# Five expert pairs' outputs through DRAM rows instead of one-hot products, and a third weight load under way, in a decoder layer with a mixture of experts

## The chip, the cores and the metric

One core of a Trainium2 chip runs the whole layer as one program. The metric is device time in microseconds: the median of three runs of the kernel before is 706.11 us (704.12 to 707.72). TensorE is called PE here, VectorE DVE, ScalarE ACT, GpSimd POOL, and SyncE, which only issues DMAs, SP.

## The reference, cut to what matters

A decoder layer on 512 tokens of 1024 float32 channels: two attention branches, then a mixture of 32 experts of which each token takes two, then a final norm. The change is in the mixture, of which the reference does this:

```python
g_sel = jnp.argmax(g_logits, axis=-1)            # one of 4 groups
top_vals, top_idx = lax.top_k(e_in, 2)           # two of its 8 experts
weight = p_group * jax.nn.softmax(top_vals, axis=-1)
expert_id = g_sel[:, None] * 8 + top_idx
...
def expert_block(args):                          # the tokens of one expert
    xb, e = args
    return (jax.nn.silu(xb @ w_g[e]) * (xb @ w_u[e])) @ w_d[e]
...
out = jnp.zeros((T, D)).at[slot_tok].add(ys * slot_w[:, None])
```

Each expert has three weights of 1 MB (two of 1024x256, one of 256x1024), so the mixture reads 96 MB. x is then x plus this sum, and the result is its rmsnorm.

## The kernel before, in words

Up to about 436 us the kernel computes the attention branches, their merge and the router. From there `experts` (L819) works through the 32 experts as 16 pairs q = 0 to 15. A pair has 128 slots: 64 partitions for each of its two experts, one row of x per slot. On 512 tokens with two choices over 32 experts, some half of the slots hold a token. In a pair, PE does in this order (the order on PE and POOL is written out by hand, `manual_schedule` at L826; on the other engines a planner sets it):

1. `gate_up` (L760): 32 products for G, 32 for U (line 769), from the transposed rows xT and the two experts' weights. ACT makes silu of G (L774), for which it needs the slot's norm factor r from the small tile sw; DVE multiplies with U into a (L775).
2. `some(5)`: five `combine` calls (L811) that belong to the pair before. A combine is two products of a one-hot matrix S (token by slot, made by `one_hot`, L806) with the pair's outputs y, split in a high and a low part (L815 and L816), and an addition of the 128x512 result to x2 by DVE (L817). A pair has eight: four token tiles t times two halves of the channels.
3. `act_T` (L778): two transposes of a (L781), copied back by ACT (L783).
4. `some(3)`: the other three combines.
5. `next_rows` (L851): eight transposes (L746) of the next pair's gathered rows xg into xT, scaled by ACT (L753) and DVE (L754).
6. `down` (L786): 16 products with the down weights in two halves (L795). Of each half ACT writes the weighted high part (L802) and DVE the low part (L803).

POOL copies the slot weights of a pair into sw (`slot_weights`, L733: two copies of 64 partitions, L738, and one of 128, L739), and after `next_rows` it issues two indirect DMAs (`gather_rows`, L723, line 728) that fetch the rows of pair q + 2: xg, 4 KB for each slot that holds a token, and wg, 132 bytes for each. Slots without a token have an index out of bounds and are skipped. xg has one buffer, so a gather waits until the transposes of the rows before have read it.

The weights come through SP. `new_w` (L669) hands out 20 buffers of 1 MB (NH) in a ring: load n takes the buffer of load n - 20, that is of a weight some three pairs earlier. `load` (L678) also makes load n wait until load n - 2 has landed, so that two are under way. After pair 15, `last` (L876) does its combines, the norm and the store.

The tiles that stay (constants, router results) come from the pool `const`, and small rotating ones from `small`; the pool of big tiles begins in memory behind them.

Of the kernel before, what the change touches and what calls it, by code (L numbers as in the profile page):

```python
# [10 lines left out]
F32 = mybir.dt.float32  # L11
# [3 lines left out]
I32 = mybir.dt.int32  # L15
U32 = mybir.dt.uint32
AF = mybir.ActivationFunctionType
ALU = mybir.AluOpType
# [3 lines left out]
P = 128  # L22
T = 512
NT = T // P
D = 1024
# [5 lines left out]
NEG = -1e30  # L31
NE = 32
NH = 20


class Layer:
# [84 lines left out]
    def setup(self):  # L121
        nc, tc, ctx, io = self.nc, self.tc, self.ctx, self.io
        self.const = ctx.enter_context(tc.tile_pool(name="const", bufs=1, side="left"))
        self.small = ctx.enter_context(tc.tile_pool(name="small", bufs=1, side="left"))
        self.big = ctx.enter_context(tc.tile_pool(name="big", bufs=16, side="left"))
        c = self.const
        self.ident = c.tile([P, P], F32, name="ident")
        make_identity(nc, self.ident)
        self.mhalf = c.tile([P, 1], F32, name="mhalf")
        nc.gpsimd.memset(self.mhalf, -0.5)  # L130
        self.eps = c.tile([P, 1], F32, name="eps")
        nc.gpsimd.memset(self.eps, EPS * D)

    def load_consts(self):
# [495 lines left out]
    def route_setup(self):  # L630
        nc, tc, io, c = self.nc, self.tc, self.io, self.const
        self.dram = dp = self.ctx.enter_context(tc.tile_pool(name="dram", bufs=1, space=bass.MemoryType.DRAM))
        self.x2d = dp.tile([T, D], F32, name="x2d")
        self.Wd = dp.tile([T, NE + 1], F32, name="Wd")
        self.wr = c.tile([P, KD, 40], F32, name="wr")
        nc.gpsimd.memset(self.wr, 0.0)
        self.load_late(self.wr[:, :, 0:4], io["w_router_group"][0].rearrange("(j p) g -> p j g", p=P))
        for g in range(4):
            self.load_late(self.wr[:, :, 8 + 8 * g:16 + 8 * g],
                              io["w_router_expert"][0, g].rearrange("(j p) e -> p j e", p=P))  # L640
        self.gpj = c.tile([P, KD], F32, name="gpj")
        self.load_late(self.gpj, io["ffn_norm"][0].rearrange("(p j) -> p j", p=P))
        self.gcol = gcol = c.tile([P, KD], F32, name="gcol")
        self.load_late(gcol, io["ffn_norm"][0].rearrange("(j p) -> p j", p=P))
        nc.vector.tensor_scalar(self.gpj, self.gpj, 32.0, None, ALU.mult)
        nc.vector.tensor_scalar(gcol, gcol, 32.0, None, ALU.mult)
        nc.vector.tensor_tensor(self.wr, self.wr, gcol.unsqueeze(2).to_broadcast([P, KD, 40]), ALU.mult)
        self.rb = c.tile([P, 40], F32, name="rb")
        nc.gpsimd.memset(self.rb, -3e38)
        self.load_late(self.rb[:, 0:4], io["b_router_group"][0:1, :].to_broadcast([P, 4]))  # L650
        self.load_late(self.rb[:, 8:40], io["b_router_expert"].rearrange("o g e -> o (g e)")
                          .to_broadcast([P, 32]))
        self.rc = c.tile([P, 33 + NT], F32, name="rc")
        self.load_late(self.rc, io["rconst"])
        self.iota32 = self.rc[:, 0:32]
        self.slot = self.rc[:, 32:33]
        self.token = self.rc[:, 33:33 + NT]
        self.tri = c.tile([P, 2, P], F16, name="tri")
        self.after(nc.gpsimd.dma_start(self.tri, io["tri"]), self.started)
        self.tm = c.tile([P, T], F16, name="tm")  # L660
        self.after(nc.gpsimd.dma_start(self.tm, io["tm"]), self.started)
        self.M = c.tile([P, NT, NE], F16, name="M")
        self.sq = c.tile([P, 2, NT], F32, name="sq")
        self.W = c.tile([P, NT, NE + 1], F32, name="W")
        self.iotaU = c.tile([P, NE], U32, name="iotaU")
        nc.vector.tensor_copy(self.iotaU, self.iota32)


    def new_w(self):  # L669
        i = self.nw % NH  # L670
        self.nw += 1
# [5 lines left out]

    def load(self, dst, src):  # L678
        d = self.nc.sync.dma_start(dst, src)
        if len(self.loads) >= 2:  # L680
            self.after(d, self.loads[-2])
        self.loads.append(d)

    def load_w(self, src, how):
# [126 lines left out]
    def combine(self, S, y, half, t):  # L811
# [4 lines left out]
        nc.tensor.matmul(cp, S[:, t * P:(t + 1) * P], y[1], start=False, stop=True)  # L816
        nc.vector.tensor_tensor(self.x2[t][:, hs], self.x2[t][:, hs], cp, ALU.add)  # L817

    def experts(self):  # L819
        nc, tc = self.nc, self.tc  # L820
        NP = NE // 2
        wgu, wd = {}, {}
        for q in range(3):
            wgu[q], wd[q] = self.load_gu(q), self.load_d(q)
        self.yhl = self.wp.tile([P, 2048], F32R, name="yhl", tag="whi")
        with tc.manual_schedule(engines={mybir.EngineType.PE, mybir.EngineType.Pool}):  # L826
            xT, sw, xg = {0: self.xT0}, {}, {}
            S, y, todo = None, None, []
            for q in range(NP):
                if q > 0 and q + 2 < NP:  # L830
                    wgu[q + 2], wd[q + 2] = self.load_gu(q + 2), self.load_d(q + 2)
                    if q + 2 == NP - 1:
                        self.load_final()
                if q:
                    sw[q] = self.slot_weights(q, wg, nc.gpsimd)

                def some(n):
                    for _ in range(min(n, len(todo))):
                        self.combine(S, y[todo[0][0]], *todo[0])
                        todo.pop(0)  # L840

                def between(j):
                    if q == 0 and j == 3:
                        self.tokens()
                        xg[1] = self.gather_rows(self.xi[:, 1:2], self.rows)
                    if q == 0 and j == 5:
                        sw[0] = self.take_weights()
                    if q == 0 and j == 9:
                        self.count_blocks()
                a = self.gate_up(wgu.pop(q), xT.pop(q), lambda: sw[q][1], between)  # L850
                def next_rows():  # L851
                    xT[q + 1] = self.new_xT()
                    for g in range(2):
                        self.gathered_T(xg[q + 1][0], xT[q + 1], g)
                if q == 0:
                    next_rows()
                some(5)
                aT = self.act_T(*a)
                some(3)
                if 0 < q < NP - 1:  # L860
                    next_rows()
                if q + 1 < NP:
                    wg = xg.pop(q + 1)[1]
                if q + 2 < NP:
                    xg[q + 2] = self.gather_rows(self.xi[:, q + 2:q + 3])
                S = self.one_hot(self.xf[:, q:q + 1])
                dn = wd.pop(q)
                y = [None, None]
                todo = [(h, t) for h in range(2) for t in range(NT)]
                if q == NP - 1:  # L870
                    self.last(S, dn, aT, sw[q][0])
                    break
                for h in range(2):
                    y[h] = self.down(dn, aT, sw[q][0], h)
# [158 lines left out]
class Route:  # L1033
# [60 lines left out]
    def choose_experts(self):  # L1094
        nc, L = self.nc, self.L
        self.v8, vi = self.tmp("v8", [8]), self.tmp("vi", [8], U32)
        nc.vector.max(self.v8, self.es)
        nc.vector.max_index(vi, self.v8, self.es)
        self.Mk = self.tmp("Mk", [2, NE])
        nc.vector.tensor_tensor(self.Mk, L.iotaU.unsqueeze(1).to_broadcast([P, 2, NE]),  # L1100
                                vi[:, 0:2].unsqueeze(2).to_broadcast([P, 2, NE]), ALU.is_equal)
        nc.vector.tensor_tensor(L.M[:, self.t], self.Mk[:, 0], self.Mk[:, 1], ALU.add)
# [15 lines left out]

    def places(self):
        nc, L, t, N = self.nc, self.L, self.t, self.N  # L1120
        n = self.tmp("n", [2])
        for c in range(2):
            nc.vector.scalar_tensor_tensor(self.es, self.Mk[:, c], 1.0, N, ALU.mult, ALU.mult, accum_out=n[:, c:c + 1])
        self.at(self.AB[:, :, 0:64], n)
# [33 lines left out]
def shape_consts():  # L1158
    out = {}
# [8 lines left out]
    q = np.arange(P)[:, None]  # L1168
    c = np.arange(T)[None, :]
# [2 lines left out]
    tri[:, 0] = np.arange(P)[:, None] <= np.arange(P)[None, :]  # L1172
    tri[:, 0] += 1024.0 * np.eye(P)
    out["tri"] = tri
    rc = np.zeros((P, 33 + NT), np.float32)
    rc[:, 0:32] = np.arange(32)
    rc[:, 32] = 1025 + np.arange(P) % 64
    rc[:, 33:] = np.arange(P)[:, None] + P * np.arange(NT)[None, :] - 1024
    out["rconst"] = rc
    out["tm"] = np.broadcast_to(np.arange(T, dtype=np.float32) - 1024, (P, T)).copy()  # L1180
    return out
# [30 lines left out]
```

## Time and profile before

| | |
|---|---|
| runs, median of 3 | 706.11 us |
| profiled execution, its own time | 705.33 us |
| its span, first to last instruction | 703.5 us |
| mean granted TensorE clock | 0.992 |
| PE busy | 683.6 us (97%) |
| DVE, ACT, POOL busy | 57%, 39%, 10% |
| DMA moved | 148.17 MB, mean 211 GB/s |

All times inside the trace count from the span's first instruction. The profiled execution's time is 1.83 us over its span, and 0.78 us under the median. A mean duration of matmuls is longer than their spacing, since they overlap: how far apart they start is read from a timeline. The DMA share is the part of the time that packets took on the core's 16 DMA engines; it can pass 1.00 a little, since a packet counts where it starts.

### The profile page before, as it was taken

The numbers are of one execution on the slowest core, as the hardware profiler recorded it, in microseconds if no ns is written. First come the engines' busy times: TensorE is split into PE (matmuls) and PEld (weight loads), VectorE is DVE, ScalarE is ACT, GpSimd is POOL, SyncE is SP. The second block draws the span as 40 slices with busy tenths as digits, with TensorE's granted clock in tenths as the row PEclk, the third lists the DMA queues.
The fourth block names the chain that finished last, engine by engine and source line by source line (L and its number), as shares of the span: only waits on it lengthen the run. The fifth ranks groups of instructions, "written<-read, shape, count | busy, mean of one in ns | idle before, by whom it ended". The sixth has DMA issues, their size and how long they took to land.

```text
span 703.5 us, 11377 instructions
## 1 busy us (share of the span) xinstructions
PE 683.6 (97%) x4262; PEld 522.5 (74%) x4262; DVE 398.8 (57%) x972; ACT 277.3 (39%) x623; POOL 70.9 (10%) x151
## 2 busy tenths in 40 slices
PE   8999999999999999999999999999999999999991
PEld 7998887777788888888888998566656666666651
DVE  5535956877829964423765317255555544555545
ACT  5747544555638663422333334211212111212123
POOL 1404000000000000000000012211121111111103
PEclk9999999999999999999999999999999999999996
DMA  8725431110272144212789758898999999999923
GB/s 256 152 61 90 106 121 60 61 49 13 68 171 61 27 156 119 61 61 94 262 301 352 287 189 315 316 361 308 377 364 393 392 394 355 372 377 348 367 89 122
DMA packets 73786, 148.17 MB, mean 211 GB/s; under 512 B 30938, under 2 KB 53554, under 8 KB 61952
## 3 DMA queue, kind: packets, MB, share of 16 engines
q1 hardware_dynamic: 67616, 138.69, 56.1%
q10 hardware_dynamic: 3040, 4.27, 2.3%
q0 software_dynamic: 3072, 4.46, 2.1%
q8 instruction: 35, 0.57, 0.3%
q14 instruction: 23, 0.19, 0.1%
HBM read 145.35 MB, written 4.26 MB: 213 GB/s over the span
## 4 chain that ended last, share of the span: by engine, by line
PE 88%; DMA 4%; issue 3%; DVE 2%; ACT 1%; POOL 1%; SPq 0%; POOLq 0%; DVEq 0%; ACTq 0%
PE yp L795 7%; PE G L769 6%; PE U L769 6%; PE pacc L96 5%; PE pacc L95 5%; PE pacc L94 5%; PE pacc L448 4%; PE pacc L447 4%; PE pacc L449 4%; PE cp L815 4%; PE cp L816 3%; PE ptr L420 3%; DMA wg<-Wd,xi 3%; PE S L402 2%; PE O L428 2%
## 5 line engine op out<-in xcount | busy, mean ns | idle before, releaser
L65 DVE SCALAR_TENSOR_TENSOR wlo<-wraw,ms,whi 128x256 fp32r<-128x256 f32 (+2 forms) x134 | 68.3, 552 | 31.4 <-ACT whi L64 31.2
L64 ACT ACTIVATE whi<-wraw,ms 128x256 fp32r<-128x256 f32 (+2 forms) x134 | 67.0, 559 | 42.1 <-PE pacc L448 20.1
L817 DVE TENSOR_TENSOR x<-x,cp 128x512 f32<-128x512 f32 x128 | 78.1, 682 | 0.8 <-PE cp L816 0.8
L94 PE MATMUL pacc<-whi,hThi 128*128 128x352 f32 (+1 forms) x192 | 72.6, 378 | 0.0
L95 PE MATMUL pacc<-wlo,hThi 128*128 128x352 f32 (+1 forms) x192 | 70.6, 369 | 0.0
L96 PE MATMUL pacc<-whi,hTlo 128*128 128x352 f32 (+1 forms) x192 | 70.5, 367 | 0.0
L775 DVE SCALAR_TENSOR_TENSOR a<-U,sw,a 128x256 f32<-128x256 f32 x16 | 11.0, 685 | 84.9 <-PE U L769 62.0
L795 PE MATMUL yp<-w,a 128*64 128x512 f32 x256 | 58.5, 598 | 0.5 <-ACT a L783 0.5
L769 PE MATMUL G<-w,xT 128*64 128x256 f32 x512 | 58.3, 380 | 0.0
L769 PE MATMUL U<-w,xT 128*64 128x256 f32 x512 | 58.2, 379 | 0.0
L769 PEld LDWEIGHTS G<-w,xT 128*64 128x64 f32 x512 | 36.5, 137 | 24.6 <-issue 4.6
L815 PE MATMUL cp<-yhl,S 128*128 128x512 f32 x128 | 53.6, 419 | 0.2 <-DVE x L817 0.2
L816 PE MATMUL cp<-yhl,S 128*128 128x512 f32 x128 | 50.8, 396 | 0.8 <-DVE yhl L803 0.8
L447 PE MATMUL pacc<-hThi,whi 128*128 128x512 f32 x128 | 50.6, 396 | 0.0
L448 PE MATMUL pacc<-hTlo,whi 128*128 128x512 f32 x128 | 50.4, 394 | 0.0
L769 PEld LDWEIGHTS U<-w,xT 128*64 128x64 f32 x512 | 36.7, 137 | 18.4
L449 PE MATMUL pacc<-hThi,wlo 128*128 128x512 f32 x128 | 50.1, 392 | 0.0
L415 ACT ACTIVATE E<-E,mx 128x128 f32<-128x128 f32 (+3 forms) x64 | 35.6, 557 | 20.5 <-DVE mx L412 19.7
L803 DVE SCALAR_TENSOR_TENSOR yhl<-yp,sw,yhl 128x512 fp32r<-128x512 f32 x32 | 24.0, 751 | 31.3 <-ACT yhl L802 31.3
L802 ACT ACTIVATE yhl<-yp,sw 128x512 fp32r<-128x512 f32 x32 | 22.0, 687 | 47.4 <-PE yp L795 47.4
L94 PEld LDWEIGHTS pacc<-whi,hThi 128*128 128x128 f32 x192 | 36.1, 188 | 5.2 <-issue 1.3
L95 PEld LDWEIGHTS pacc<-wlo,hThi 128*128 128x128 f32 x192 | 36.1, 188 | 4.5 <-issue 0.7
(221 smaller groups left out, 1307.8 us busy)
## 6 DMA issues: line engine op xcount, KB each, us to landing
w<-in_w_exp_gate_dram SPq DMA_DIRECT2D x32, 1024.0 KB, 6.1
w<-in_w_exp_up_dram SPq DMA_DIRECT2D x32, 1024.0 KB, 6.1
w<-in_w_exp_down_dram SPq DMA_DIRECT2D x30, 1024.0 KB, 5.8
wraw<-in_w_in_dram SPq DMA_DIRECT2D x14, 1024.0 KB, 5.3
wraw<-in_w_out_dram SPq DMA_DIRECT2D x4, 1024.0 KB, 7.1
wraw<-in_w_in_dram SPq DMA_DIRECT2D x5, 704.0 KB, 4.8
xs<-in_x_dram SPq DMA_DIRECT2D x4, 512.0 KB, 6.6
wraw<-in_w_o_mla_dram SPq DMA_DIRECT2D x4, 512.0 KB, 3.4
```

Source lines behind the costliest of these rows:

```text
L65: nc.vector.scalar_tensor_tensor(lo[:, k], raw[:, k], g, hi[:, k].bitcast(F32), ALU.mult, ALU.subtract)
L94: nc.tensor.matmul(ps[t][:, :ncols], act_hi[kk // 4][:, kk % 4, ts], hi[:, k], start=kk == 0, stop=False)
L95: nc.tensor.matmul(ps[t][:, :ncols], act_hi[kk // 4][:, kk % 4, ts], lo[:, k], start=False, stop=False)
L96: nc.tensor.matmul(ps[t][:, :ncols], act_lo[kk // 4][:, kk % 4, ts], hi[:, k], start=False, stop=kk == ktot - 1)
L447: nc.tensor.matmul(ps, hi[:, k, ds], self.hT[0][k // 4][:, k % 4], start=k == 0, stop=False)
L448: nc.tensor.matmul(ps, hi[:, k, ds], self.hT[1][k // 4][:, k % 4], start=False, stop=False)
L449: nc.tensor.matmul(ps, lo[:, k, ds], self.hT[0][k // 4][:, k % 4], start=False, stop=k == KD - 1)
L769: nc.tensor.matmul(GU[i][es, 0:256], xT[:, j, es], gu[e][i][:, j * 256:(j + 1) * 256], start=j == 0, stop=j == KD - 1)
L795: nc.tensor.matmul(yp[es], aT[:, j, es], wd[e][:, j * D + half * 512:j * D + half * 512 + 512], start=j == 0, stop=j == 1)
L815: nc.tensor.matmul(cp, S[:, t * P:(t + 1) * P], y[0], start=True, stop=False)
L816: nc.tensor.matmul(cp, S[:, t * P:(t + 1) * P], y[1], start=False, stop=True)
L817: nc.vector.tensor_tensor(self.x2[t][:, hs], self.x2[t][:, hs], cp, ALU.add)
```

## The change

Pairs 1, 3, 5, 7 and 9 (`VIA`) no longer combine. `down_out` lets ACT write the weighted outputs of both halves into a 128x1024 tile y, and POOL issues a DMA that writes y (512 KB) into its 128 rows of a new DRAM tensor yd. S, the high and low parts and the eight combines of these pairs go. In pairs 10 to 13, `take_slots` fetches, for token tile t = q - 10 and for each of the two choices, the rows of yd that belong to the tile's tokens: POOL fills a 128x1024 tile with zeros and issues an indirect DMA; tokens whose choice is not in those five pairs have an index out of bounds. One pair later, DVE adds the two tiles to x2. The rows' numbers are worked out once by DVE in `slot_rows`, in pair 1, from the router's masks Mk and places, which are now kept for all token tiles in `const`. The combines that are left are spread: in pairs 1 to 10 four of them instead of eight, two ahead of `act_T` and two behind it. A load waits for the load three before it. The constant table rc is longer by 32 columns, and a tile `pad` of 24 floats is put behind `eps`.

```diff
+VIA = (1, 3, 5, 7, 9)
...
+        c.tile([P, 24], F32, name="pad")
...
     def load(self, dst, src):
         d = self.nc.sync.dma_start(dst, src)
-        if len(self.loads) >= 2:
-            self.after(d, self.loads[-2])
+        if len(self.loads) >= 3:
+            self.after(d, self.loads[-3])
...
+    def slot_rows(self):
+        nc, c = self.nc, self.const
...
+        for t in range(NT):
+            for i in range(2):
+                nc.vector.scalar_tensor_tensor(junk, self.Mk[:, t, i], 1.0, self.base, ALU.mult, ALU.mult,
+                                               accum_out=rows[:, t, i:i + 1])
+        nc.vector.tensor_scalar(far, self.place, 1088.5, float(1 << 20), ALU.is_gt, ALU.mult)
+        nc.vector.tensor_tensor(rows, rows, self.place, ALU.add)
+        self.yi = c.tile([P, NT, 2], I32, name="yi")
+        nc.vector.tensor_tensor(self.yi, rows, far, ALU.add)
+
+    def down_out(self, wd, aT, sw, q):
+        nc = self.nc
+        y = self.bl.tile([P, D], F32, name="y", tag="yd", bufs=2)
+        for h in range(2):
+            nc.scalar.mul(y[:, h * 512:h * 512 + 512], self.down_products(wd, aT, h), sw)
+        i = VIA.index(q) * P
+        nc.gpsimd.dma_start(self.yd[i:i + P], y)
+
+    def take_slots(self, t, i):
+        nc = self.nc
+        y = self.bl.tile([P, D], F32, name="y", tag="yd", bufs=2)
+        nc.gpsimd.memset(y, 0.0)
+        nc.gpsimd.indirect_dma_start(out=y, out_offset=None, in_=self.yd,
+                                     in_offset=bass.IndirectOffsetOnAxis(ap=self.yi[:, t, i:i + 1], axis=0),
+                                     bounds_check=len(VIA) * P - 1, oob_is_err=False)
+        return t, y
...
-                some(5)
+                n = min(len(todo), 4) if VIA[0] <= q <= VIA[-1] + 1 else len(todo)
+                some((n + 1) // 2 + (n > 4))
                 aT = self.act_T(*a)
-                some(3)
+                some(n // 2 - (n > 4))
...
                 if q + 2 < NP:
                     xg[q + 2] = self.gather_rows(self.xi[:, q + 2:q + 3])
+                if q == 1:
+                    self.slot_rows()
+                for t, r in taken:
+                    nc.vector.tensor_tensor(self.x2[t], self.x2[t], r, ALU.add)
+                t = q - VIA[-1] - 1
+                taken = [self.take_slots(t, i) for i in range(2)] if 0 <= t < NT else []
+                dn = wd.pop(q)
+                if q in VIA:
+                    self.down_out(dn, aT, sw[q][0], q)
+                    continue
                 S = self.one_hot(self.xf[:, q:q + 1])
```

## Rows read from the trace of the kernel before

**Rows 1.** The page: busy time of PE, then the span in 40 slices of 17.6 us (GB/s of all DMAs), then the queue of POOL's DMAs (packets, MB, share of 16 engines).

```profile
PE 683.6 (97%) x4262; PEld 522.5 (74%) x4262; DVE 398.8 (57%) x972; ACT 277.3 (39%) x623; POOL 70.9 (10%) x151
...
GB/s 256 152 61 90 106 121 60 61 49 13 68 171 61 27 156 119 61 61 94 262 301 352 287 189 315 316 361 308 377 364 393 392 394 355 372 377 348 367 89 122
...
q0 software_dynamic: 3072, 4.46, 2.1%
```

**Rows 2.** PE's timeline of one pair (start us, duration us, engine, line, operation), weight loads left out: the first two and the fifth product of the combines, the transposes of a, the transposes of the next rows, and the down products.

```profile
598.53 0.50 PE L815 MATMUL cp<-yhl,S 128*128 128x512 f32 x1
598.87 0.40 PE L816 MATMUL cp<-yhl,S 128*128 128x512 f32 x1
...
599.57 0.39 PE L815 MATMUL cp<-yhl,S 128*128 128x512 f32 x1
...
600.96 0.38 PE L781 MATMUL G<-ident,a 128*128 128x128 f32 x2
...
602.58 1.31 PE L746 MATMUL ptr<-ident,xg 128*128 128x128 f32 x8
603.82 3.65 PE L795 MATMUL yp<-w,a 128*64 128x512 f32 x16
```

**Rows 3.** The chain that ended last, in order of time: the G products of pair 4 and of pair 15.

```profile
497.73 3.45 PE G L769 x32
...
670.03 3.45 PE G L769 x32
```

**Rows 4.** Stretches of the expert stage: us; busy time of PE, PEld, DVE, ACT, POOL with counts; then granted clock, DMA share, GB/s.

```profile
440.00:460.00 20.00, 19.54 (x148) 12.00 (x145) 7.34 (x18) 4.03 (x8) 3.94 (x7) 1.00 0.90 321
460.00:475.00 15.00, 15.00 (x104) 9.24 (x103) 7.63 (x14) 2.87 (x6) 2.61 (x5) 1.00 0.96 367
475.00:497.50 22.50, 22.29 (x139) 13.04 (x139) 13.40 (x24) 4.79 (x10) 4.85 (x8) 1.00 0.90 329
497.50:655.00 157.50, 157.50 (x1070) 98.83 (x1068) 82.75 (x141) 31.36 (x61) 26.05 (x50) 1.00 0.97 374
655.00:675.30 20.30, 20.30 (x154) 12.92 (x152) 9.03 (x15) 4.89 (x9) 0.84 (x5) 1.00 0.83 310
```

**Rows 5.** Who SP's weight loads waited for: us in total, times, longest.

```profile
SPq L679 <- DMA w<-in_w_exp_gate_dram: 87.9, 28, 8.7
SPq L679 <- DMA w<-in_w_exp_up_dram: 77.4, 29, 5.2
SPq L679 <- DMA w<-in_w_exp_down_dram: 69.4, 29, 3.6
...
SPq L679 <- PE cp L816: 3.0, 12, 0.3
```

**Rows 6.** SP's timeline: the gate loads of pair 4 and of pair 15, and the last load of all (the down weights of pair 15 come in four loads of half the size, this is the fourth).

```profile
453.52 3.59 SPq L679 DMA_DIRECT2D w<-in_w_exp_gate_dram  x2
...
651.30 2.82 SPq L679 DMA_DIRECT2D w<-in_w_exp_gate_dram  x2
...
669.33 0.55 SPq L679 DMA_DIRECT2D w<-in_w_exp_down_dram  x1
```

**Rows 7.** From issue to landing (min, median, max us) of the loads: the very last one, issued at 669.33, and the 66 issued between 459 and 655 us. Then PE's down products of pair 15.

```profile
DMA to landing us min/median/max: 6.0/6.0/6.0
...
DMA to landing us min/median/max: 4.9/5.8/8.8
...
681.02 3.65 PE L795 MATMUL yp<-w,a 128*64 128x512 f32 x16
```

**Rows 8.** Two stretches with the same columns as rows 4: one with up to four loads of 1 MB under way (weights of the experts and of the merge together), and one with two.

```profile
372.40:388.70 16.30, 16.30 (x72) 13.06 (x71) 7.12 (x10) 3.98 (x6) 0.00 (x0) 1.00 0.99 363
...
504.60:514.60 10.00, 10.00 (x56) 6.12 (x56) 7.71 (x14) 2.70 (x6) 2.24 (x3) 1.00 1.01 408
```

**Rows 9.** Timelines of POOL, ACT and DVE around the same pair as rows 2; in brackets the idle time before and what ended it.

```profile
589.71 1.03 POOL L728 DMA_INDIRECT wg<-Wd,xi  x1 [0.30 <-issue]
590.75 0.19 POOL L738 COPY sw<-wg 64x1 f32<-64x1 f32 x1
597.72 0.18 POOL L738 COPY sw<-wg 64x1 f32<-64x1 f32 x1 [6.78 <-DMA wg<-Wd,xi]
597.96 0.18 POOL L739 COPY sw<-wg 128x1 f32<-128x1 f32 x1
...
591.83 0.69 ACT L802 ACTIVATE yhl<-yp,sw 128x512 fp32r<-128x512 f32 x1 [1.06 <-PE yp L795]
598.18 0.72 ACT L774 ACTIVATE a<-G,sw 128x256 f32<-128x256 f32 x1 [5.66 <-POOL sw L739]
...
598.93 0.69 DVE L775 SCALAR_TENSOR_TENSOR a<-U,sw,a 128x256 f32<-128x256 f32 x1 [5.63 <-ACT a L774]
```

**Rows 10.** Groups of instructions (count, busy us, mean ns), and DMA issues (count, KB each, median us to landing).

```profile
L817 DVE TENSOR_TENSOR x<-x,cp 128x512 f32<-128x512 f32 x128 | 78.1, 682 | 0.8 <-PE cp L816 0.8
L475 DVE TENSOR_TENSOR gate<-gate 128x512 f32<-128x512 f32 x8 | 5.5, 688 | 0.1
L619 POOL MEMSET xg<- 128x1024 f32 x1 | 0.9, 947 | 0.0
...
x2d<-x ACTq DMA_DIRECT2D x4, 384.0 KB, 5.4
xg<-x2d,xi POOLq DMA_INDIRECT x15, 6.9
```

More of the change, by code (lines that the diff above doesn't have):

```diff
@@ L633, in route_setup @@
         self.x2d = dp.tile([T, D], F32, name="x2d")
+        self.yd = dp.tile([len(VIA) * P, D], F32, name="yd")
         self.Wd = dp.tile([T, NE + 1], F32, name="Wd")
@@ L652, in route_setup @@
                           .to_broadcast([P, 32]))
-        self.rc = c.tile([P, 33 + NT], F32, name="rc")
+        self.rc = c.tile([P, 33 + NT + NE], F32, name="rc")
         self.load_late(self.rc, io["rconst"])
@@ L657, in route_setup @@
         self.token = self.rc[:, 33:33 + NT]
+        self.base = self.rc[:, 33 + NT:]
         self.tri = c.tile([P, 2, P], F16, name="tri")
@@ L662, in route_setup @@
         self.M = c.tile([P, NT, NE], F16, name="M")
+        self.Mk = c.tile([P, NT, 2, NE], F32, name="Mk")
+        self.place = c.tile([P, NT, 2], F32, name="place")
         self.sq = c.tile([P, 2, NT], F32, name="sq")
@@ L817, in combine @@
         nc.vector.tensor_tensor(self.x2[t][:, hs], self.x2[t][:, hs], cp, ALU.add)
+    def slot_rows(self):
+        nc, c = self.nc, self.const
+        rows = c.tile([P, NT, 2], F32, name="yrows")
+        far = c.tile([P, NT, 2], F32, name="far")
+        junk = c.tile([P, NE], F32, name="yjunk")
+        for t in range(NT):
[21 more added lines that the diff above has]
+        return t, y
     def experts(self):
@@ L827, in experts @@
             xT, sw, xg = {0: self.xT0}, {}, {}
-            S, y, todo = None, None, []
+            S, y, todo, taken = None, None, [], []
             for q in range(NP):
@@ L865, in experts @@
                     xg[q + 2] = self.gather_rows(self.xi[:, q + 2:q + 3])
+                if q == 1:
[8 more added lines that the diff above has]
+                    continue
                 S = self.one_hot(self.xf[:, q:q + 1])
-                dn = wd.pop(q)
                 y = [None, None]
@@ L1098, in choose_experts @@
         nc.vector.max_index(vi, self.v8, self.es)
-        self.Mk = self.tmp("Mk", [2, NE])
+        self.Mk = L.Mk[:, self.t]
         nc.vector.tensor_tensor(self.Mk, L.iotaU.unsqueeze(1).to_broadcast([P, 2, NE]),
@@ L1120, in places @@
         nc, L, t, N = self.nc, self.L, self.t, self.N
-        n = self.tmp("n", [2])
+        n = L.place[:, t]
         for c in range(2):
@@ L1174, in shape_consts @@
     out["tri"] = tri
-    rc = np.zeros((P, 33 + NT), np.float32)
+    rc = np.zeros((P, 33 + NT + NE), np.float32)
     rc[:, 0:32] = np.arange(32)
     rc[:, 32] = 1025 + np.arange(P) % 64
-    rc[:, 33:] = np.arange(P)[:, None] + P * np.arange(NT)[None, :] - 1024
+    rc[:, 33 + NT:] = [64 * (2 * VIA.index(i // 2) + i % 2) - 1025 if i // 2 in VIA else 1 << 20 for i in range(NE)]
+    rc[:, 33:33 + NT] = np.arange(P)[:, None] + P * np.arange(NT)[None, :] - 1024
     out["rconst"] = rc
```

## The prediction, made before the changed kernel ran

> **What bounds the kernel now.** I read the page first: PE is busy 97% of the span, and from slice 24 on the DMAs move 308 to 394 GB/s, more than anywhere before [rows 1]. So the expert stage, the only one that the change touches beyond a few small tiles, has two loads near their limit at once, and the question is which of them sets its end. For PE I read a pair's timeline and the chain: the chain of pairs 4 to 15 is nothing but PE, and a pair takes (670.03 - 497.73) / 11 = 15.66 us [rows 3]. For the DMAs I read SP: the gate loads of pair 4 are issued at 453.52 and those of pair 15 at 651.30, which is 197.78 / 11 = 17.98 us for a pair [rows 6]. So the loads are the slower of the two. They start well ahead, 497.73 - 453.52 = 44.2 us before their products, and end 670.03 - 651.30 = 18.7 us ahead. SP's waits say what holds them: 234.7 us for the landing of another load against 3.0 us for the combines that free a buffer [rows 5]. PE lives on a lead that it uses up at 2.3 us a pair. At the end little is left: the last load lands at 669.33 + 6.0 = 675.3, and its half of the down products begins at 681.02 + 1.83 = 682.85 [rows 6, 7]. **The slack is 7.5 us.** PE cannot end earlier by more than that unless the stream of loads ends earlier too.
>
> **PE's side of the sum.** Removed are 40 combines, 80 products. Within a run of combines the second and the fifth product start at 598.87 and 599.57, so 0.233 us apart (the 0.4 us of a row is longer, since they overlap) [rows 2]. 80 x 0.233 = 18.7 us less, spread as 1.87 us over each of pairs 1 to 10. Nothing is added on PE. The 40 DVE additions that go (0.68 us each) and the new ones (8 of 128x1024, by twice 0.69 us for 128x512 in SBUF, 1.4 us each, 11 us) hang on an engine that is busy 82.75 of 157.50 us [rows 4, 10]; I cost them at nothing, as long as their rows have landed, and a pair passes in between. slot_rows is some eleven short DVE instructions, hidden likewise. The pad, the longer table, Mk and places only move addresses: nothing, and no row could show otherwise.
>
> What comes back on PE are waits for a, and here POOL matters. In the pair shown, U's last products end about when the first combine starts, at 598.53; a is ready at 598.93 + 0.69 = 599.62, and the five combines cover this until 600.96 [rows 2, 9]. With two combines the transposes would want it at 598.53 + 0.94 = 599.47: 0.15 us late, 1.5 us over ten pairs. But POOL was the late one already: its second copy into sw waits 6.78 us, until the gather issued just before it has landed, and only then come silu (0.72) and a [rows 9]. I read this as: that copy waits for everything that POOL has in its queue. Then a write of yd holds it too. Its y is complete at 591.83 + 0.69 = 592.52; POOL's issue lies at once behind; landing after 5.4 us, as 384 KB from ACT's queue took, up to 5.4 x 512 / 384 = 7.2 us [rows 10], so at 598.0 to 599.8 instead of 597.72. With 0.46 us to silu and 1.44 us through silu and a (as in rows 9: 597.72 to 598.18, 598.18 to 599.62), a comes at 599.9 to 601.7, 0.4 to 2.2 us too late. I take 1.3, for five pairs 6.5 us. The fetches: behind wg's issue, which ends at 590.74, two memsets of 0.95 and two issues of 1.03, each with some 0.3 us around it, put the second fetch's issue at about 594.0 and its landing, by 5.4 to 6.9 us, at 599.4 to 600.9; a comes at 601.3 to 602.8, while the five combines of pairs 11 to 14 last until 600.96. That is 0.3 to 1.8 us, I take 1.1, for four pairs 4.4 us. If the copy does not wait for them, both are nothing. **PE's own end moves by -18.7 + 1.5 + 6.5 + 4.4 = -6.3 us**, between -17.2 and -18.7 + 1.5 + 11 + 7.2 = +1.0.
>
> **The loads' side.** Added traffic: five writes of 0.524 MB, 2.62 MB; eight fetches in which only the tokens of ten of the 32 experts move, 1024 x 10 / 32 = 320 rows of 4 KB, 1.31 MB. Together 3.93 MB. At the 374 GB/s of the long stretch [rows 4] this is 10.5 us; at the best stretch's 408 GB/s [rows 8] 9.6 us. It could cost more: today's six loads of a pair, at the best spacing 4.9 / 2 = 2.45 us each [rows 7], would take 14.7 of the 17.98 us, and if all of the other 3.3 us were the doing of the gather, which moves about 4.1 / 15 = 0.28 MB [rows 1], the price would be 12 us for a MB and the sum 46 us. But 363 GB/s also stands in a stretch ahead of the first gather [rows 8], so I take 10.5 and keep up to 20 for the range.
>
> The writes ride on POOL's queue, beside SP's. The Trainium skill's page "DMA: Bandwidth & Descriptors" (section "Issuing engines are not separate DMA queues") has a rule against this part of the change: DMAs of every issuing engine run on the same 16 DMA engines and interleave. The trace agrees, a share of 0.97 over 157.5 us with both queues at work [rows 4]; by the rule the writes cost the loads their bytes, without it writes and fetches would cost the loads nothing, and their sum would be 10.5 us lower.
>
> The third load can only fill what is idle. By the DMA shares that is 20.0 x 0.10 + 15.0 x 0.04 + 22.5 x 0.10 + 157.5 x 0.03 + 20.3 x 0.17 = 13.0 us up to 675.3 [rows 4]. Against much more speaks that up to four loads under way gave 363 GB/s and two gave 408 [rows 8], though those four had shorter pieces; for some speaks that the lowest shares stand where loads are few or small, at 440 to 460 and at the end, where two halves under way are 1 MB. From 0 to 13 I take 7.5. **The last landing then moves by +10.5 - 7.5 = +3.0 us, and with 7.5 us of slack used up PE ends 4.5 us earlier.** That PE frees buffers earlier doesn't help: hardly a wait for a buffer ends last [rows 5].
>
> **Sum.** The later of the two ends counts, the loads' -4.5 against PE's -6.3. The tail behind the down products stays. From the profiled execution's 705.33 us this is 700.8; the median stands 0.78 us above that execution, so I forecast 706.11 - 4.5 = 701.6 us.
>
> **The rivals.**
> *The third load is worth all of the idle time and POOL's copy waits for nothing new.* Then the loads end at -7.5 + 10.5 - 13.0 = -10 us and PE at -17.2, so the kernel at 696. For it: shares of 0.83 and 0.90 in 63 us of the stage. Against it: rows 8, and the copy's wait in rows 9. A stream that is faster still would leave PE's own limit, 706.11 - 17.2 = 689.
> *The traffic wins: slower.* Place: the loads of pairs 12 to 15. If the 13 new transfers cost 20 us and the third load gives nothing, the stream ends 20 us later, PE waits for the down weights of pair 15 and ends +12.5 us: 718.6; it decides from the point where traffic minus the third load's gain exceeds the 7.5 us of slack. Halfway, at 14 and 0, it is 712.6. For it: 0.97 share already. Against: 13 us of idle share.
> *POOL's wait takes the place of the combines.* If landings of writes and fetches take 2 us longer than I took, nine pairs lose 18 us more and PE ends at -6.3 + 18 = +11.7 us, 717.8; at 0.7 us longer it is no change, 706. It would show as idle PE ahead of L781 in pairs 2 to 14. The Trainium skill's "GPSIMD Engine Reference" (section "Specifications") says that GpSimd's port to SBUF is shared with VectorE when a DVE instruction has two SBUF inputs; no row here shows what that costs, and the new additions are of that kind.
> *It does no more than move waits about:* traffic and third load cancel to the 7.5 us of slack, 706.
>
> **Chances.** Forecast (loads set the end, 698 to 706): 0.42, of which 0.28 lie more than 0.5% faster. All of the idle time used: 0.12, faster. Traffic: 0.20, of which 0.14 slower. POOL: 0.16, of which 0.10 slower and 0.02 faster. Nothing: 0.10, of which 0.08 within and the rest to either side. A measurement of this kernel can tell about 0.5%, 3.5 us, from no change. Together: faster 0.43, same 0.32, slower 0.25. The likeliest case's own range is 698 to 706; from the costs' ends (689 and 718) I cut what the tails leave, one in ten on each side: 694 to 712.
>
> **What would show it.** Right: pairs 1 to 10 take about 14 us where nothing waits; SP has three loads under way, and its waits are still for landings; the DMA share over 497 to 655 is nearer 1.0, at no more than some 385 GB/s; PE's idle time lies ahead of G, U or down products in the last four pairs and its releaser is a weight load; the last load lands at about 678. POOL's L738 copies would begin at landings of yd. Wrong: loads that wait for buffers to the end (then PE is the bound and rows 5 misled me); PE idle ahead of L781 for 2 us and more in each pair; a rate well over 400 GB/s in the long stretch (then the third load is worth more); a last landing behind 683 (then it is slower).

## The result and the profile after

The changed kernel takes 713.21 us (median; 711.16 to 713.70) against 705.75 us for the kernel before beside it (704.12 to 707.72): a ratio of 1.0096, with a 95% interval of 1.0067 to 1.0126. It is slower by about 1%, where 701.6 us was forecast. The profiled execution after takes 711.16 us with a span of 709.4 us, 5.83 us over the profiled one of before.

The page of the changed kernel, to be held against [rows 1]: PE's busy time, the granted clock and the GB/s in slices of 17.7 us, and POOL's DMA queue.

```profile
PE 671.5 (95%) x4182; PEld 510.5 (72%) x4182; DVE 376.5 (53%) x944; ACT 277.5 (39%) x623; POOL 91.9 (13%) x172
...
PEclk9999999999999999999999999999999999888997
...
GB/s 256 150 61 89 105 120 60 60 61 1 90 154 54 61 120 119 76 43 118 264 278 381 248 232 271 407 413 415 419 413 411 415 416 415 414 417 358 65 1 122
...
q0 software_dynamic: 4944, 8.35, 3.5%
```

PE is busy 12 us less, with 80 products fewer, and 3.89 MB more go through POOL's queue, as the change says. Two things are new. From slice 26 to 36 the DMAs move 407 to 419 GB/s, where they moved 308 to 394, and then they are done: 65 and 1 GB/s in slices 38 and 39. The loads have finished long before the end. And PE's clock, full over the whole stage before [rows 4], is down in three slices, 35 to 37 (602 to 656 us).

The expert stage of the changed kernel, in the columns of [rows 4]: first the long stretch, then four short ones in pair 11.

```profile
497.50:655.00 157.50, 139.66 (x945) 85.91 (x941) 62.69 (x102) 28.84 (x56) 38.79 (x62) 0.94 1.01 409
...
590.00:598.00 8.00, 8.00 (x64) 5.13 (x60) 0.60 (x1) 0.00 (x0) 2.50 (x4) 1.00 1.02 412
598.00:604.00 6.00, 0.03 (x1) 0.00 (x0) 1.21 (x3) 0.70 (x1) 0.37 (x2) 0.70 1.02 421
604.00:608.00 4.00, 3.88 (x13) 3.14 (x14) 3.60 (x6) 0.38 (x1) 0.00 (x0) 0.60 1.02 424
608.00:612.00 4.00, 4.00 (x23) 1.78 (x24) 3.65 (x7) 1.31 (x3) 2.66 (x2) 1.00 1.00 414
```

PE was busy all 157.50 us of the long stretch before; now 18 us of it are idle. Six of them lie in one piece, from 598 to 604, and in the 4 us behind it the granted clock is 0.60 on average, between its two levels of 1.2 and 2.4 GHz; 13 products start there, and 23 in the 4 us after, at full clock.

What holds PE there is read from the timelines of the four engines at the same place, in the form of [rows 9]; the sixth line is from the view of line 744 (590 to 602 us) and gives the shortest, median and longest time, in ns, that POOL's sequencer spent waiting for a semaphore ahead of a copy.

```profile
587.11 1.00 POOL L734 DMA_INDIRECT wg<-Wd,xi  x1 [0.30 <-issue]
589.35 1.00 POOL L854 DMA_INDIRECT y<-yd,yi  x1 [0.27 <-POOL y L853]
591.58 1.00 POOL L854 DMA_INDIRECT y<-yd,yi  x1 [0.27 <-POOL y L853]
592.59 0.19 POOL L744 COPY sw<-wg 64x1 f32<-64x1 f32 x1
601.59 0.18 POOL L744 COPY sw<-wg 64x1 f32<-64x1 f32 x1 [8.81 <-DMA y<-yd,yi]
...
L744 POOLq EVENT_SEMAPHORE  x2: 17/3122/6227, 594.6 to 595.3; - x2
...
602.06 0.70 ACT L780 ACTIVATE a<-G,sw 128x256 f32<-128x256 f32 x1 [12.24 <-POOL sw L745]
602.79 0.66 DVE L781 SCALAR_TENSOR_TENSOR a<-U,sw,a 128x256 f32<-128x256 f32 x1 [12.19 <-ACT a L780]
603.30 1.86 DVE L823 TENSOR_TENSOR x<-x,cp 128x512 f32<-128x512 f32 x3
...
588.89 3.62 PE L775 MATMUL G<-w,xT 128*64 128x256 f32 x32
...
597.63 0.40 PE L822 MATMUL cp<-yhl,S 128*128 128x512 f32 x1
...
604.12 0.77 PE L821 MATMUL cp<-yhl,S 128*128 128x512 f32 x1 [6.09 <-DVE x L823]
...
612.17 3.62 PE L775 MATMUL G<-w,xT 128*64 128x256 f32 x32
```

Follow it from the top. POOL issues the gather of pair 12 and then the two fetches, the last at 591.58. The second copy into sw, which pair 11 needs, starts only at 601.59, when that fetch has landed, 9.9 us after its issue. This wait is in the program: POOL's sequencer stands 6.23 us in one wait instruction ahead of that copy, and the semaphores for which the trace has the copy wait are those of pair 12's gathers and of both fetches, although it reads none of what they bring; why the program has these waits is open. Silu and a come behind it at 602.06 and 602.79. DVE works in order, and the additions of the combines stand behind a in its queue; four combines (eight products, the last at 597.63) fill the four PSUM tiles into which combines write, and the fifth waits for the first addition, until 604.12. So the combines can't cover a late a beyond the fourth. Then the products of 128x512 follow each other at 0.43 us (606.81 to 607.24 in the trace) instead of 0.233 for 3 us. The pair takes 23.28 us, from the first G product at 588.89 to the next pair's at 612.17, where it took 15.64 before. The next two do the same (23.52 each); the fourth, whose fetches are issued when the loads are over, takes 16.51.

The groups of the changed kernel show the same as sums: the releaser behind the last bar of each line, with the idle time it ended.

```profile
L781 DVE SCALAR_TENSOR_TENSOR a<-U,sw,a 128x256 f32<-128x256 f32 x16 | 10.9, 682 | 125.7 <-ACT a L780 112.7
...
L821 PE MATMUL cp<-yhl,S 128*128 128x512 f32 x88 | 41.0, 466 | 18.2 <-DVE x L823 18.2
...
L780 ACT ACTIVATE a<-G,sw 128x256 f32<-128x256 f32 x16 | 11.4, 712 | 102.2 <-POOL sw L745 96.7
```

Only L821's 18.2 us are PE's, and they are three quarters of the 24 us that these four pairs lose; the idle times of ACT and DVE are long but mostly beside PE's work.

The account of the 5.8 us by which PE's last down products start later (689.90 against 684.08), from the starts of the G products: the experts begin 1.59 us later (437.51 against 435.92), pairs 1 to 10 take 137.37 instead of 157.38 us (-20.01), pairs 11 to 14 take 86.83 instead of 62.56 (+24.27), pairs 0 and 15 the same. So the change wins what it promised in ten pairs, and loses it and more in the four that fetch.

### The profile page after: what moved, and what is told of

It is laid out like the page before. It is cut to its first block, busy times and chain, and to the rows that moved or that the text cites. A ratio compares the mean times of both kernels' runs of the same rounds, so it can differ in the third digit from the quotient of the medians.

```text
span 709.4 us, 11085 instructions
## 1 busy us (share of the span) xinstructions
PE 671.5 (95%) x4182; PEld 510.5 (72%) x4182; DVE 376.5 (53%) x944; ACT 277.5 (39%) x623; POOL 91.9 (13%) x172
## 4 chain that ended last, share of the span: by engine, by line
PE 65%; DMA 16%; issue 10%; POOL 4%; DVE 2%; ACT 2%; SPq 0%; POOLq 0%; ACTq 0%; DVEq 0%
DMA wg<-Wd,xi 11%; PE pacc L97 5%; PE pacc L96 5%; PE pacc L95 5%; PE pacc L451 4%; PE pacc L449 4%; PE pacc L450 4%; DMA y<-yd,yi 4%; PE ptr L422 3%; PE S L404 2%; PE O L430 2%; PE pacc L493 2%; PE pacc L474 2%; PE pacc L473 2%; PE pacc L475 2%
## 5 line engine op out<-in xcount | busy, mean ns | idle before, releaser
L821 PE MATMUL cp<-yhl,S 128*128 128x512 f32 x88 | 41.0, 466 | 18.2 <-DVE x L823 18.2
L823 DVE TENSOR_TENSOR x<-x,cp 128x512 f32<-128x512 f32 x88 | 54.8, 680 | 2.3 <-PE cp L822 2.1
L780 ACT ACTIVATE a<-G,sw 128x256 f32<-128x256 f32 x16 | 11.4, 712 | 102.2 <-POOL sw L745 96.7
L821 PEld LDWEIGHTS cp<-yhl,S 128*128 128x128 f32 x88 | 18.1, 206 | 29.5 <-issue 25.6
```

What stands on the lines that cost most here:

```text
L821: nc.tensor.matmul(cp, S[:, t * P:(t + 1) * P], y[0], start=True, stop=False)
```

## The experiments

Theory W: the fetches, indirect DMAs in POOL's queue, hold the second copy into sw, and that alone is the loss. Rival A: the new additions of whole rows on DVE hold the combines. Rival L: loads and traffic set the end.

**The copies ahead of the fetches (e1_sw_early).** POOL's list is changed at one place: the weights of the next pair are copied before this pair's gather and fetches are issued.

```
-                if q:
+                if q and q not in sw:
                     sw[q] = self.slot_weights(q, wg, nc.gpsimd)
...
                 if q + 1 < NP:
                     wg = xg.pop(q + 1)[1]
+                    if q:
+                        sw[q + 1] = self.slot_weights(q + 1, wg, nc.gpsimd)
                 if q + 2 < NP:
```

> The changed kernel with one move: slot_weights of the next pair is put on POOL's list ahead of this pair's gather and fetch issues, so that its copies stand behind the gather of a pair earlier, not behind the indirect DMAs just issued. Theory W (POOL's copy into sw waits for the landing of the indirect DMAs queued ahead of it, silu and a come late, PE stands and its clock falls): the stalls of pairs 10 to 13 go, pairs 11 to 13 take about 15.7 us instead of 23.5, and the time falls by 18 to 22 us to about 691 (profiled pairs 1 to 9 stay at 13.7). Rival A (the additions of fetched rows on DVE, 1.2 us each and two a pair, hold the combines' additions and so the PSUM buffers): the time stays within 3 us of 713. Rival L (the loads and the new traffic set the end): within 3 us of 713 too, with PE waiting ahead of G or U for a weight load.

Measured: 686.82 us, a ratio to the kernel before of 0.9712 (0.9688 to 0.9737). By the profiled executions that is 24.8 us under the changed kernel (711.16 - 686.41), more than the 18 to 22 expected. Pairs 1 to 10 take 13.66 us each and pairs 11 to 14 15.64, and of PE's waits in the expert stage 1.2 us are left. POOL's timeline of this kernel at the same place, then ACT's two silus of pairs 11 and 12:

```profile
590.72 1.00 POOL L854 DMA_INDIRECT y<-yd,yi  x1 [0.27 <-POOL y L853]
594.28 0.18 POOL L744 COPY sw<-wg 64x1 f32<-64x1 f32 x1 [2.57 <-DMA wg<-Wd,xi]
600.31 0.18 POOL L744 COPY sw<-wg 64x1 f32<-64x1 f32 x1 [5.84 <-DMA y<-yd,yi]
...
591.80 0.72 ACT L780 ACTIVATE a<-G,sw 128x256 f32<-128x256 f32 x1 [2.85 <-PE G L775]
607.44 0.72 ACT L780 ACTIVATE a<-G,sw 128x256 f32<-128x256 f32 x1 [2.79 <-PE G L775]
```

The wait is not gone: the second copy still stands 5.84 us behind a fetch. But it now copies the weights of pair 12, whose silu wants them at 607.44; silu follows G, not POOL. W holds, A and L fall: additions and traffic are all still there.

**No fetches (e2_no_fetch).** The eight indirect DMAs are left out; the memsets and the additions stay, so the five pairs' part is missing from the output.

```
         nc.gpsimd.memset(y, 0.0)
-        nc.gpsimd.indirect_dma_start(out=y, out_offset=None, in_=self.yd,
...
         return t, y
```

> The changed kernel without the eight fetches: the memsets of y and the additions stay, so zeros are added and the five pairs' part is left out of the output. Theory W: the stalls of pairs 10 to 13 go, since only the gather of xg and wg is left ahead of the copy; the copy waits 5 to 7 us as in the kernel before, and the time is 690 to 694. Rival A (the additions): no change, 713 within 3 us. Rival L: 1.3 MB less traffic, 3.5 us at 374 GB/s, so about 709.

Measured: 690.33 us, ratio 0.9760 (0.9728 to 0.9793). W again. POOL's waits of this kernel in the expert stage (us in total, times, longest):

```profile
POOL sw L744 <- DMA wg<-Wd,xi: 70.8, 15, 7.3
```

The copy is back to waiting for the gather alone. That this is still 3.5 us slower than the kernel above fits a gather's wait that shows where there are fewer combines: three of pairs 1 to 10 take 14.2 to 14.4 us instead of 13.66, and in each PE stands 0.3 to 0.5 us ahead of the transposes of a. Why two of the last ones take 15.9 and 16.0 instead of 15.64 is open.

**Two loads under way, with the copies ahead (e3_sw_early_2loads).** The kernel of the first experiment with the third load undone.

```
-        if len(self.loads) >= 3:
-            self.after(d, self.loads[-3])
+        if len(self.loads) >= 2:
+            self.after(d, self.loads[-2])
```

> As e1_sw_early, but with two loads under way as in the kernel before. If the third load is what took the loads off the end (the long stretch went from 374 to 409 GB/s with it), the loads now set it: the last landing comes about 10 us later than the 675.3 of the kernel before, for 3.9 MB more at 374 GB/s, and the time is 706 to 711, some 17 us over e1_sw_early. If the third load does nothing and the loads only ran faster because PE freed their buffers sooner, the time is that of e1_sw_early within 2 us.

Measured: 728.33 us, ratio 1.0295 (1.0254 to 1.0337): worse than either end expected. What PE waits for in this kernel's expert stage, up to 690 us:

```profile
PE U L775 <- DMA w<-in_w_exp_up_dram: 19.1, 11, 3.8
PE G L775 <- DMA w<-in_w_exp_gate_dram: 4.4, 3, 2.3
```

That is what a bound by the loads looks like; in the changed kernel PE waits for no load there.

**The third load alone (e4_before_3loads),** in the kernel before (the same two lines, the other way).

> The kernel before with three loads under way and nothing else. Its PE takes 15.64 us a pair with a lead in the loads until the end, so if PE sets the end it stays at 705.8 within 2 us, while the last load is issued some 12 to 17 us earlier than 669.3. It also shows whether the 1.6 us that the changed kernel's experts start later come from the third load (then this kernel is slower by about that). If instead the loads set the end of the kernel before, it gains 5 us or more.

Measured: 707.70 us, ratio 1.0012 (0.9987 to 1.0036): no change, with the last load issued 26 us earlier (12 to 17 were expected). PE set the end of the kernel before. The experts of this kernel begin at 435.94, so the 1.6 us are not the third load's.

**Two loads, no traffic (e8_2loads_no_yd).** The kernel with two loads, less the five writes and the eight fetches (the five pairs' part is left out).

```
-        i = VIA.index(q) * P
-        nc.gpsimd.dma_start(self.yd[i:i + P], y)
...
-        nc.gpsimd.indirect_dma_start(out=y, out_offset=None, in_=self.yd,
```

> e3_sw_early_2loads without the five writes of yd and the eight fetches (memsets and additions stay, the five pairs' part is left out of the output). It asks why two loads under way, which gave 374 GB/s in the kernel before, give 332 to 352 in e3. Theory T (the new transfers between the loads cost them far more than their 3.9 MB): the last load is issued at 665 to 672 as in the kernel before, not at 698.9, and the time is 698 to 704. Rival B (the faster pairs of PE take SBUF or buffers from the loads): the last load is issued behind 685 and the time is over 715.

Measured: 707.08 us (the median of ten, from 698.11 to 715.99), ratio 0.9947 (0.9901 to 0.9994); the profiled execution takes 700.5 us. Its last load is issued at 671.94, as theory T has it, but the median time is 3 us above T's range. Why its executions lie so far apart is open, and the profiled one is among the fastest.

With the first, third, fourth and fifth experiment and both kernels there is a table of when the last load is issued, each from SP's timeline of the profiled execution, with the rate from 500 to 581 us:

| | two loads under way | three loads under way |
|---|---|---|
| without the writes and fetches | 669.33 (before), 671.94; 381 and 360 GB/s | 643.51; 414 GB/s |
| with them | 698.87; 332 GB/s | 655.92 (652.13 in the changed kernel); 412 and 414 GB/s |

Here are the row of SP for three loads and no traffic, and then the one for two loads and traffic, each followed by the stretch from 500 to 581 us and the landing times of the loads issued in it (min, median, max); last, these landing times for two loads without traffic (e8_2loads_no_yd):

```profile
643.51 0.54 SPq L679 DMA_DIRECT2D w<-in_w_exp_down_dram  x1
...
500.00:581.00 81.00, 80.83 (x550) 49.78 (x547) 41.25 (x70) 15.48 (x30) 13.07 (x25) 1.00 1.01 414
...
DMA to landing us min/median/max: 7.2/8.1/8.6
```

```profile
698.87 0.55 SPq L685 DMA_DIRECT2D w<-in_w_exp_down_dram  x1
...
500.00:581.00 81.00, 73.33 (x488) 42.72 (x487) 26.09 (x44) 15.41 (x30) 14.04 (x27) 0.96 0.93 332
...
DMA to landing us min/median/max: 5.8/7.2/8.8
...
DMA to landing us min/median/max: 4.8/6.1/7.5
```

The third load is worth 25.8 us without the traffic (669.33 - 643.51) and 43 with it (698.87 - 655.92); the traffic costs 12.4 us with three loads (655.92 - 643.51) and 26.9 with two (698.87 - 671.94). Each figure is from single executions; of the 12.4, 1.5 are the later start of the experts, and 3.93 MB at 412 GB/s would be 9.5. The landings fit that the two don't add. With two under way the spacing of loads is about half a landing: 6.1 / 2 = 3.05 us without the traffic, and 7.2 / 2 = 3.6 us with it, when the writes lengthen the landings (no fetch of this kernel falls in that stretch). With three it is 8.1 / 3 = 2.7, and the DMA engines are full (share 1.01), so that little more than the bytes should count. The Trainium skill's page "DMA: Bandwidth & Descriptors" (section "Where 436 GB/s comes from") gives a ceiling of 435 GB/s for a core's path into SBUF; the most that a stretch of the changed kernel shows is 424.

**Four loads under way (e9_sw_early_4loads),** in the kernel of the first experiment.

```
-        if len(self.loads) >= 3:
-            self.after(d, self.loads[-3])
+        if len(self.loads) >= 4:
+            self.after(d, self.loads[-4])
```

> e1_sw_early with four loads under way. Three already keep the DMA engines at a share of 1.01 over 500 to 581 us, at 412 GB/s. If that is the limit, the rate stays within 2% of 412, the last load is issued at 655.9 within 3 us and the time is 687 within 2 us. If every load under way more gives rate, as from two to three, the last load is issued 5 us earlier or more; the time would still be PE's, 686 to 687. If landings of the gathers grow behind more loads, it gets slower by some us.

Measured: 686.17 us, ratio 0.9719 (0.9697 to 0.9740), the last load at 655.69, 417 GB/s from 500 to 581: three loads had filled the DMA engines. The landings only grew, to 11.1 us in the median, and 11.1 / 4 = 2.8 us is again the spacing.

**The pad (e6_sw_early_no_pad, e7_sw_early_pad480).** The kernel of the first experiment without the pad of 96 bytes, and then with 480 bytes.

```
-        c.tile([P, 24], F32, name="pad")
```

> e1_sw_early without the pad of 96 bytes: every tile of the big pool moves down by 96 bytes. The changed kernel's experts begin 1.6 us later than those of the kernel before, all of it lost between 254 and 376 us, where products of 128x512 follow each other at 0.233 us instead of 0.229. Theory P (where the big pool's tiles lie sets that spacing): the first G product moves by some tenths of a us to 3 us from 437.4, either way. Rival: addresses do nothing, and the 1.6 us come from the new instructions on DVE: G stays at 437.4 within 0.2 us. In either case the time stays at 687 within 4 us.

```
-        c.tile([P, 24], F32, name="pad")
+        c.tile([P, 120], F32, name="pad")
```

> e1_sw_early with a pad of 480 bytes instead of 96, so that the big pool's tiles lie exactly 1024 bytes behind those of the kernel before, where they lie 640 bytes behind it in the changed kernel. Theory P: the spacing between 254 and 376 us is again that of the kernel before, G begins at 436 and the time falls by 1 to 2 us to about 685. Rival: no change, G at 437.4.

Measured: 689.05 us without (688.88 to 689.23; ratio 0.9759, 0.9738 to 0.9781), 685.45 us with 480 bytes (684.62 to 686.48; ratio 0.9714, 0.9689 to 0.9739). The first G product lies at 440.42, 437.40 and 436.07 us without a pad, with 96 and with 480 bytes; before it was 435.92. Theory P: PE's timeline of the same products of 128x512, first in the changed kernel, then with 480 bytes.

```profile
320.32 0.39 PE L449 MATMUL pacc<-hThi,whi 128*128 128x512 f32 x1
...
321.02 0.40 PE L449 MATMUL pacc<-hThi,whi 128*128 128x512 f32 x1
...
321.73 0.39 PE L449 MATMUL pacc<-hThi,whi 128*128 128x512 f32 x1
```

```profile
320.20 0.39 PE L449 MATMUL pacc<-hThi,whi 128*128 128x512 f32 x1
...
320.89 0.39 PE L449 MATMUL pacc<-hThi,whi 128*128 128x512 f32 x1
...
321.58 0.39 PE L449 MATMUL pacc<-hThi,whi 128*128 128x512 f32 x1
```

Three products take 0.705 us in the one and 0.69 in the other, 2%; the 120 us of such products in this part of the kernel make some 2 us of that. Theory P holds for the spacing: between 256 and 376 us its mean is 0.229 us in every trace with 480 bytes and in every trace of the kernel before and its variants, and 0.233 in every trace with 96 bytes and in the one without a pad. The start of the experts is a weaker sign. Without a pad 1.3 us more are lost before 13 us, but 1.2 and 1.5 us are lost there too in the traces of e9_sw_early_4loads and e5_before_sw_early, whose edits don't touch that part, and e5's experts begin at 437.44 with the addresses of the kernel before. 480 bytes give the lowest median of this study, by less than its spread.

**The copies ahead, in the kernel before (e5_before_sw_early):** the two edits of the first experiment on the kernel before.

> The kernel before with slot_weights of the next pair put ahead of this pair's gather on POOL's list, and nothing else. In the kernel before POOL's second copy waits 5 to 7 us for the gather's landing too, but five combines cover it and every pair takes 15.64 us. Theory W: the wait there is hidden, so nothing changes: 706 within 2 us and 15.64 us a pair. Rival: part of a pair's 15.64 us is already that wait, and the gain of e1_sw_early is mostly not the change's: then this kernel gains 5 us or more.

Measured: 706.69 us, ratio 1.0012 (0.9983 to 1.0042), and 15.64 us a pair (read from the slowest of its ten executions, 712.75 us, the profiled one), as theory W has it: POOL's wait for the gather cost the kernel before nothing, since five combines covered it.

**Six pairs through DRAM (e10_six_pairs),** on top of the 480 bytes.

```
-VIA = (1, 3, 5, 7, 9)
+VIA = (1, 3, 5, 7, 8, 9)
```

> e7_sw_early_pad480 with six pairs through DRAM: 1, 3, 5, 7, 8 and 9. It asks what bounds the good version. PE: eight combines less, 16 x 0.233 = 3.7 us, but pairs 9 and 10 then have no combine to cover the wait for a, 1 to 1.5 us each. Loads: 0.52 MB written and 0.26 MB fetched more, at 12.4 us for 3.93 MB (e4 against e1) 2.5 us later. If PE alone is the bound: 1 us faster than e7, 684.5. If the loads are, with some 2 us between the last landing and its use in e7: no change to 1 us slower, 685 to 687. Both within 2 us of 685.5; the trace tells by the wait ahead of the last down products and of G and U.

Measured: 686.15 us, ratio 0.9725 (0.9706 to 0.9743): nothing gained. Of the 3.7 us that the products are worth, pairs 9 and 10 keep 1.65, since no combine covers a late a there. The last load is issued at 656.26, 2.6 us later than with five, and pairs 12 to 14 take 16.75 us instead of 15.64. PE's waits for a from 560 to 670 us, and its timeline in one of the pairs 12 to 14:

```profile
PE G L787 <- DVE a L781: 2.0, 2, 1.2
...
620.89 0.59 PE L775 MATMUL U<-w,xT 128*64 128x256 f32 x2
621.97 3.67 PE L775 MATMUL U<-w,xT 128*64 128x256 f32 x30 [0.48 <-DMA w<-in_w_exp_up_dram]
```

U's third product stands behind its weights. So the loads hold this kernel in its late pairs, and at 410 to 415 GB/s (600 to 651 us) they are within 2% of what four loads under way gave; by this one step, five pairs are about where both sides meet.

## Why the prediction was wrong

**What bounds the kernel: right as far as it went.** PE set the end of the kernel before with the loads not far behind; the third load alone moved the loads by 26 us and the time by nothing.

**PE's removed products: right.** -18.7 us taken; pairs 1 to 10 take 136.63 us with the copies ahead, against 157.38 before, -20.75, of which about 1 us are longer pairs in the kernel before (157.38 against ten of 15.64).

**The cover by two combines, and the writes: too dear.** 1.5 + 6.5 us were taken; in the changed kernel pairs 1 to 10 take 137.37 us, 0.7 more than with the copies ahead, for both terms together. The reading of [rows 9], that the copy waits for everything in POOL's queue, was wrong for the plain write. POOL's timeline of pair 1 in the changed kernel, and then the landing of the write in it:

```profile
466.40 0.59 POOL L847 DMA_DIRECT2D yd<-y  x1 [2.04 <-ACT y L845]
467.00 0.20 POOL L744 COPY sw<-wg 64x1 f32<-64x1 f32 x1
471.57 0.18 POOL L744 COPY sw<-wg 64x1 f32<-64x1 f32 x1 [4.37 <-DMA wg<-Wd,xi]
...
DMA to landing us min/median/max: 8.8/8.8/8.8
```

The write lands at 475.2, and the copy starts at 471.57 without it, behind the gather. Only indirect DMAs hold the copy here: the semaphores for which the trace has it wait are the gathers', and the write's is not among them.

**The fetches: the step that failed.** 1.1 us in each of four pairs, 4.4 us; measured 24.3 us. The mechanism and its place were the prediction's own; three sizes in it were off. The landing was taken from medians, 5.4 to 6.9 us [rows 10], and took 8.0 to 9.9 beside three loads, which the same change brings; with two loads it was 7.9 in the median, and 3.4 for the fetch behind the last load. The prediction's own [rows 9] already had a gather that let the copy go 8.0 us after its issue (589.71 to 597.72). The cover was taken to reach to the fifth combine, and the additions' place behind a in DVE's queue ends it after the fourth. And 6 us of idle PE cost more than 6: of the 24.3 us, 18.2 are idle, and most of the other 6 are products at the lower clock. In pair 11, where 1.1 us were taken and 7.6 measured, the landing makes about 4 us of the difference and the cover and the clock 1 to 1.5 each.

**The loads' side: wrong in both terms, and they were added.** The traffic was taken at 10.5 us (up to 20), the third load at -7.5 (0 to -13); as they stand together, the last load is issued 17.2 us earlier, not 3 us later. SP's row in the changed kernel, against the 669.33 of [rows 6]:

```profile
652.13 0.54 SPq L685 DMA_DIRECT2D w<-in_w_exp_down_dram  x1
```

The third load's range came from idle shares of the DMA engines. That bounds what can be gained only if a busy engine moves all it can: a share of 0.97 went with 374 GB/s and a share of 1.01 with 409. The prediction's own sign for a third load worth more, a rate well over 400 GB/s in the long stretch, is there. So the loads did not set the end, and the sum took the wrong one of its two sides.

**The pad: put at nothing.** Addresses were said to cost nothing. The experts begin 1.59 us later, and 480 bytes instead of 96 give back 1.3 of it (437.40 to 436.07).

**The rivals.** What came was "POOL's wait takes the place of the combines", at 0.16: its place and its sign, through four pairs instead of nine and at about 6 us a pair. "All of the idle time used" was the loads' true side: its 689 us is near the 686.8 us that the copies ahead give. "The traffic wins" happens with two loads, at 728 us.

## What to carry to other kernels

Before indirect DMAs go onto the queue of an engine, look at what stands behind them there; if it is a small copy that the next stage wants, put it ahead, where its wait lies beside other work: here one moved call turned 1% slower into 3% faster. Take landing times at the number of transfers that will be under way after the change, not before it. When one part of a change adds traffic and another adds depth, their costs are not a sum: price the pair.

## What the runs showed of the hardware that was not expected

The number of loads of 1 MB under way sets the rate well beyond what the busy share says: two gave 374 GB/s at a share of 0.97 [rows 4], three 409 to 414 at 1.01, four 417. Two came to 408 only in a stretch of 10 us [rows 8], where the loads that landed took about the shortest time of [rows 7], 4.9 us.

After 6 us without a product PE's granted clock was below its upper level for about 3 us of work, and products of 128x512 came 0.43 us apart.

Where the operands lie in SBUF changed the mean spacing of products of 128x512 from 0.229 to 0.233 us; 384 bytes more of pad gave it back.

An indirect issue takes longer when it begins while DVE is at an addition of two SBUF operands. POOL's and DVE's timelines in the changed kernel, then the same two in e1_sw_early:

```profile
609.03 1.02 POOL L734 DMA_INDIRECT xg<-x2d,xi  x1 [7.01 <-PE ptr L752]
610.36 1.74 POOL L734 DMA_INDIRECT wg<-Wd,xi  x1 [0.30 <-issue]
...
610.01 1.22 DVE L910 TENSOR_TENSOR x<-x,y 128x1024 f32<-128x1024 f32 x1
...
601.27 1.02 POOL L734 DMA_INDIRECT xg<-x2d,xi  x1 [0.53 <-issue]
...
601.52 1.22 DVE L912 TENSOR_TENSOR x<-x,y 128x1024 f32<-128x1024 f32 x1
```

1.74 us instead of 1.00 where 0.87 us of the addition were still to come, and 1.02 where the addition began behind the issue. This agrees with the rule of the Trainium skill's "GPSIMD Engine Reference" (section "Specifications") that GpSimd's way into SBUF is shared with VectorE where an instruction of it has two SBUF inputs. Here it is 0.7 us, and in three of the four pairs it stands on the path, since the two fetches are issued behind it.
